# A fixed VectorE order between stages, two weight low parts on GpSimd and a reset bank turn in an encoder kernel

## The chip, the cores and the metric

The kernel runs on one core of a Trainium2 chip. The metric is the device time of one execution in microseconds (us); the time before is the median of three runs. Engines are called by their names in the profile: PE (TensorE), DVE (VectorE), ACT (ScalarE), POOL (GpSimd), SP (the DMA queue's engine).

## The reference, cut to what matters

Two encoder layers on 272 tokens (16 learned meta tokens ahead of 256) of 1024 channels, in float32. Each layer mixes tokens twice in parallel (chunkwise retention and windowed attention), merges both by gates, and then runs a squared-ReLU MLP. Around each half stands a norm before and a norm after:

```
u    = rms_norm(h, norm_mix_pre[l]);  proj = u @ w_in[l]
...
mix  = (sigmoid(gate_r) * y_r + sigmoid(gate_a) * y_a) @ w_mix_o[l]
h    = h + rms_norm(mix, norm_mix_post[l])
u    = rms_norm(h, norm_ff_pre[l])
ff   = square(relu(u @ w_ff1[l])) @ w_ff2[l]
h    = h + rms_norm(ff, norm_ff_post[l])
```

What matters here is the step from one product to the next: the norm after, the addition to `h`, and the input `u` of the next product.

## The kernel before, in words

Channels lie on the 128 partitions, so an activation is eight tiles of 128 channels by 272 tokens (256 in the second layer's later part). Every weight is a unit of 128 x 1024 float32, loaded through three `raw` buffers. To keep float32 precision a unit is split by `unit` (L119): ACT casts it to a high part `wh` (L131), DVE computes the low part `wl = raw - wh` (L132). Both have four buffers, so four units at most lie ready. The activation is split likewise, into `uh` (ACT, L242) and `ul` (DVE, L243, recorded at the helper's line L93). `product` (L146) makes one output tile of 128 channels from one unit: for each of the eight input tiles `mm3` (L135) issues three matmuls into one PSUM bank, wh by uh (L136), wh by ul (L137), wl by uh (L138), in that order in each bank.

Between two stages stands `leave` and then `enter`. `leave` (L296) takes the products out of PSUM (`yg`, ACT), sums squares, lets PE make the mean (L183) and run twenty small matmuls on zeros (`warm`), and gets 1/sqrt on ACT (L189, L190). A Newton step is folded into the update of `h`: its `update(k)` (L312) makes, for tile 0, the tile of `yg`, then `h`, then `y1`, and for every later tile a scaled `yg` and then `h = h + yg`. `held` (L310) makes the fourth weight unit of the next stage be cast on ACT only after the square of the 1/sqrt. `enter` (L225) runs over the eight tiles: `update(k)`, `uh` on ACT, `ul` on DVE, and the sum of squares for the next norm (`accumulate`). There are three such places: mix to ff1 in either layer, and ff2 of layer 0 to the second layer's first products. In the trace they begin at about 251, 447 and 681 us.

No order among these DVE instructions is written down. Each engine runs its instructions in one fixed order, which the framework's scheduler chose from its own estimate of times, save where `tc.issue_after` ties an instruction behind another of the same engine. The order so chosen differs from the code's: in the first place DVE does `y1` before tile 0 of `h`, and takes the later tiles often in pairs.

PSUM banks of the products go round by `wide` (L85): a counter `turn` steps through the tags "asatats" (three banks "a", two "s", two "t"). It runs on through both layers; the first output product (`att_o`, L740) of layer 0 gets "s", the next "a" and "t"; in layer 1 the first gets "a", the second "t". The steps of the retention norm before it use banks "t" and "o" too.

Of the kernel before, what the change touches and what calls it, by code (L numbers as in the profile page):

```python
# [19 lines left out]
KD = D // P  # L20
# [21 lines left out]
def encoder(ctx: ExitStack, tc: tile.TileContext, order, w, h_in, gains, dec, decm, sink, sinkm, tabs, mats, esel, masks, rel, relm, grow, out):  # L42
    nc = tc.nc
    V, A, PE, G = nc.vector, nc.scalar, nc.tensor, nc.gpsimd
    mul, add, sub, mn = ALU.mult, ALU.add, ALU.subtract, ALU.min
# [12 lines left out]
    turn = [0]  # L58
    ring.tile([P, 48], F32, name="gap", bufs=1)

    def slot(i, name, shape=(KD, T), dt=F32):
        return big.tile([P] + list(shape), dt, tag=f"b{i}", name=name)
# [7 lines left out]
    def tokens(i, name, shape=(KD,), at=32):  # L70
        return slot(i, name, (*shape, ROW), F32R)[..., at:at + T]

    def bank(tag, shape=None):
        t = psum.tile([P, 512], F32, tag=tag, name="ps_" + tag, bufs=BANKS[tag])
        if shape is None:
            return t
        n = int(np.prod(shape))
        v = t[:, :n]
        if len(shape) == 2:
            v = v.rearrange("p (a b) -> p a b", a=shape[0])  # L80
        elif len(shape) == 3:
            v = v.rearrange("p (a b c) -> p a b c", a=shape[0], b=shape[1])
        return v

    def wide():  # L85
        turn[0] += 1
        return "asatats"[turn[0] % 7]

    def f(t):
        return t.bitcast(F32)  # L90

    def stt(o, a, s, b, op0=mul, op1=mul):
        V.scalar_tensor_tensor(out=o, in0=a, scalar=s, in1=b, op0=op0, op1=op1)  # L93

    def split(xh, xl, x):
        A.activation(xh, x, AF.Copy)  # L96
# [7 lines left out]
    count = {"load": 0}  # L104
    raws = []
    held = {}

    def fetch(parts=1):
        i = count["load"]
        count["load"] += 1  # L110
        raw = ring.tile([P, D], F32, tag="raw", name="raw", bufs=3)
        n = D // parts
        cuts = [slice(j * n, (j + 1) * n) for j in range(parts)]
        raws.append((raw, cuts))
        for c in cuts:
            nc.sync.dma_start(raw[:, c], w[i][:, c])
            yield

    def unit(*name):  # L119
        i = len(order)  # L120
        order.append(name)
        if not raws:
            list(fetch())
        raw, cuts = raws.pop(0)
        wh = ring.tile([P, D], F32R, tag="wh", name="wh")
        wl = ring.tile([P, D], F32R, tag="wl", name="wl")
        for c in cuts:
            with ExitStack() as later:
                for ins in held.get(i, ()):
                    later.enter_context(tc.issue_after(ins))  # L130
                A.activation(wh[:, c], raw[:, c], AF.Copy)  # L131
                V.tensor_tensor(out=wl[:, c], in0=raw[:, c], in1=f(wh[:, c]), op=sub)  # L132
        return wh, wl

    def mm3(ps, ah, al, bh, bl, first=True, last=True):  # L135
        PE.matmul(ps, ah, bh, start=first, stop=False)  # L136
        PE.matmul(ps, ah, bl, start=False, stop=False)  # L137
        return PE.matmul(ps, al, bh, start=False, stop=last)  # L138
# [36 lines left out]
    def warm(n):  # L175
        ps = bank("t", [P])
        for _ in range(n):
            tc.keep_in_program_order(PE.matmul(ps, idle, idle, start=True, stop=True))

    def mean(parts, c0):  # L180
        ms = bank("o", [T])
        for i, p in enumerate(parts):
            PE.matmul(ms[:, c0:], mat["o1024"], p[:, c0:], start=i == 0, stop=i == len(parts) - 1)  # L183
        return ms

    def rsqrt(y1, ms, c0):
        y = two.tile([P, T], F32, tag="t1", name="y")
        w2 = two.tile([P, T], F32, tag="t2", name="w2")
        A.activation(y[:, c0:], ms[:, c0:], AF.Ln)  # L189
        A.activation(y[:, c0:], y[:, c0:], AF.Exp, scale=-0.5)  # L190
        return y, w2, newton(None if y1 is None else y1[:, c0:], ms[:, c0:], 0.0, y[:, c0:], w2[:, c0:])

    warm(WARM)
    h = const.tile([P, KD, T], F32, name="h")
    g = const.tile([P, DEPTH, 4, KD], F32, name="g")
# [24 lines left out]
    def square(src, c0):  # L220
        sq = two.tile([P, T], F32, tag="sq", name="sq", bufs=3)
        A.activation(sq[:, c0:], src, AF.Square)
        return sq

    def enter(l, n, c0, update):  # L225
        x = [tokens(i, "u" + "hl"[i], at=32 - 16 * l) for i in range(2)]
        ss = one.tile([P, T], F32, tag="ss", name="ss")

        lag = KD if n else LAG0

        def accumulate(k):
            sq = square(h[:, k, c0:], c0)
            if k == 0:
                V.tensor_scalar(out=ss[:, c0:], in0=sq[:, c0:], scalar1=8e-6, scalar2=None, op0=add)
            else:
                V.tensor_tensor(out=ss[:, c0:], in0=ss[:, c0:], in1=sq[:, c0:], op=add)

        for k in range(KD):
            if update:
                update(k)  # L240
            gk = g[:, l, n, k:k + 1]
            A.activation(x[0][:, k, c0:], h[:, k, c0:], AF.Copy, scale=gk)  # L242
            stt(x[1][:, k, c0:], h[:, k, c0:], gk, f(x[0][:, k, c0:]), op1=sub)  # L243
            if k >= lag:
                accumulate(k - lag)
        if update and n == 0:
            for k in range(KD - lag, KD):
                accumulate(k)
        return x, ss, accumulate
# [46 lines left out]
    def leave(l, n, c0, products, init=None):  # L296
        yg = slot(4, "yg")
        ss = one.tile([P, T], F32, tag="ss", name="ss2")
        for m, ps in products:
            sq = square(ps[:, c0:], c0)  # L300
            A.activation(yg[:, m, c0:], ps[:, c0:], AF.Copy, scale=g[:, l, n, m:m + 1])
            if m == 0 and init is None:
                V.tensor_scalar(out=ss[:, c0:], in0=sq[:, c0:], scalar1=8e-6, scalar2=None, op0=add)
            elif m < KD - 1:
                V.tensor_tensor(out=ss[:, c0:], in0=(init if m == 0 else ss)[:, c0:], in1=sq[:, c0:], op=add)
        y1 = one.tile([P, T], F32, tag="rb", name="y1")
        ms = mean([ss, sq], c0)
        warm(10)
        y, w2, sq = rsqrt(None, ms, c0)
        held[len(order) + 3] = [sq.ins]  # L310

        def update(k):  # L312
            yk = yg[:, k, c0:]
            if k == 0:
                V.tensor_tensor(out=yk, in0=yk, in1=y[:, c0:], op=mul)
                stt(yk, w2[:, c0:], 3.0, yk, op0=sub)
                stt(h[:, k, c0:], yk, -0.5, h[:, k, c0:], op1=add)
                stt(y1[:, c0:], w2[:, c0:], 3.0, y[:, c0:], op0=sub)
            else:
                stt(yk, yk, -0.5, y1[:, c0:])  # L320
                V.tensor_tensor(out=h[:, k, c0:], in0=h[:, k, c0:], in1=yk, op=add)

        return update

# [11 lines left out]
    lows, odds = slice(64, 128), (slice(32, 64), slice(96, 128))  # L336
# [26 lines left out]
    for l in range(DEPTH):  # L363
        c0 = 16 * l
        if l == 0:
            u, ss, early = lead()
        else:
            u, ss, _ = enter(l, 0, 0, update)
            early = [proj(u, 0, "asas"[i], "v_r", i) for i in range(4)]
# [191 lines left out]
        if l == 0:  # L561
# [6 lines left out]
            for c in range(4):  # L568
                V.tensor_tensor(
                    out=pmblk.rearrange("p (t c g k) -> p t c g k", t=4, c=4, g=2)[:, :, c],  # L570
                    in0=mat["blk"].rearrange("p (t g k) -> p t g k", t=4, g=2),
                    in1=pm[:, 0:16].unsqueeze(1).unsqueeze(1).to_broadcast([P, 4, 2, 16]),
                    op=mul,
# [163 lines left out]
                A.activation(x[:, c0:], x[:, c0:], AF.Tanh, scale=0.5)  # L737
        tc.keep_in_program_order(A.preload_act_table_set("natural_log_exp_and_others"))

        for m2 in range(4):  # L740
            wh, wl = unit("att_o", m2)
            for i in range(2):
                m = 2 * m2 + i
                ps = bank(wide(), [T])
                for k in range(4):
                    sl = slice((4 * i + k) * P, (4 * i + k + 1) * P)
                    mm3(ps[:, c0:], wh[:, sl], wl[:, sl], ao[:, 0, k, c0:], ao[:, 1, k, c0:], k == 0, k == 3)
                stt(tha[m][:, c0:], tha[m][:, c0:], 1.0, ps[:, c0:], op0=add)
# [9 lines left out]
        def mixed():  # L758
# [4 lines left out]
            for m in range(KD):  # L763
                *_, (_, ps) = pair[m] if m < 2 else product(z, c0, wide(), "mix", m)
                yield m, ps

        update = leave(l, 1, c0, mixed())

        u, ss, accumulate = enter(l, 2, c0, update)
        fs, behind = [], []  # L770

# [7 lines left out]
        for m in range(KF):  # L779
            if m % KD == 0:  # L780
                a, b = ((5, 7), (8, 9), (6, 10), (2, 3))[m // KD]
                low = [tokens(i, "fl", (4,), 32 - c0) for i in ("10a", "10b")] if b == 10 else [tokens(b, "fl", at=32 - c0)]
# [13 lines left out]
        if l == 0:  # L796
# [10 lines left out]
            update = leave(l, 3, c0, ff2(), e2)  # L807
# [180 lines left out]
```

## Time and profile before

| what | value |
|---|---|
| median of 3 runs | 868.79 us (868.16 to 870.78) |
| the profiled execution | 872.21 us, of which the span from first to last instruction is 870.4 us |
| PE busy | 852.1 us (98%) |
| DVE, ACT, POOL busy | 603.2, 559.6 and 49.9 us (69%, 64%, 6%) |
| share of the chain that ended last | PE 81%, DVE 10%, ACT 6% |
| mean granted TensorE clock | 0.996 |

The profile is of one execution. A matmul's busy time overlaps that of the next one, so PE at 98% doesn't say that PE issues at its peak; the distance from one matmul's start to the next one's says it.

### The profile page before, as it was taken

The page shows a single profiled execution, that of the slowest core. Times are in us where ns is not written, and L with a number is a line of the kernel's source. Part 1 is how long each engine was busy: PE and PEld are TensorE (multiplying, and loading weights), DVE is VectorE, ACT ScalarE, POOL GpSimd, SP SyncE. Part 2 cuts the span into 40 slices and gives each one's busy share as a digit, 9 for nine tenths or more (in the row PEclk, how much of TensorE's full clock was granted, in tenths as well). Part 3 has the DMA queues.
Part 4 walks back from the last instruction along what each step waited for, and adds up shares of the span by engine and source line. Part 5 has one row for each costly group of instructions (what it writes and reads, how often), then busy time and mean ns, then how long its engine had stood idle before and what let it go on. Part 6 is the DMA issues. An engine that isn't in the chain of part 4 may idle for free.

```text
span 870.4 us, 16670 instructions
## 1 busy us (share of the span) xinstructions
PE 852.1 (98%) x6514; PEld 819.3 (94%) x6514; DVE 603.2 (69%) x1113; ACT 559.6 (64%) x1034; POOL 49.9 (6%) x113
## 2 busy tenths in 40 slices
PE   9899999999999999999999999999999999999997
PEld 9899999999989999999989999999999999998885
DVE  7889888778768655444469898888776675554544
ACT  7448887666568777444355588886755498783432
POOL 2112220000000000000000122200000000000000
PEclk9999999999999999999999999999999999999999
DMA  8544344445545655556544544444466367666661
GB/s 294 190 123 136 118 135 131 129 155 173 169 143 171 193 173 183 178 175 186 174 121 146 155 129 154 137 139 137 121 197 198 113 214 204 196 200 192 189 193 69
DMA packets 41407, 142.15 MB, mean 163 GB/s; under 512 B 5360, under 2 KB 6256, under 8 KB 41328
## 3 DMA queue, kind: packets, MB, share of 16 engines
q1 hardware_dynamic: 40896, 140.43, 52.1%
q8 instruction: 51, 0.84, 0.4%
q10 hardware_dynamic: 432, 0.66, 0.2%
q14 instruction: 28, 0.23, 0.1%
HBM read 140.02 MB, written 1.05 MB: 162 GB/s over the span
## 4 chain that ended last, share of the span: by engine, by line
PE 81%; DVE 10%; ACT 6%; issue 1%; DMA 1%; POOL 0%; SPq 0%; DVEq 0%; ACTq 0%; POOLq 0%
PE ps_a L136 12%; PE ps_a L137 12%; PE ps_a L138 12%; PE ps_s L138 5%; PE ps_s L137 5%; PE ps_s L136 5%; PE ps_t L136 4%; PE ps_t L137 4%; PE ps_t L138 4%; DVE wl L132 3%; PE ps_a L849 2%; PE ps_s L849 2%; PE ps_s L848 2%; PE ps_a L848 2%; PE ps_a L850 2%; PE ps_s L850 2%
## 5 line engine op out<-in xcount | busy, mean ns | idle before, releaser
L132 DVE TENSOR_TENSOR wl<-raw,wh 128x1024 fp32r<-128x1024 f32 x256 | 312.8, 1223 | 198.9 <-ACT wh L131 197.3
L131 ACT ACTIVATE wh<-raw 128x1024 fp32r<-128x1024 f32 x256 | 269.9, 1058 | 203.1 <-PE ps_a L137 61.6
L136 PE MATMUL ps_a<-uh,wh 128*128 128x272 f32 (+1 forms) x912 | 265.8, 292 | 2.8 <-ACT uh L242 2.8
L138 PE MATMUL ps_a<-uh,wl 128*128 128x272 f32 (+1 forms) x912 | 259.3, 284 | 0.3 <-DVE wl L132 0.3
L137 PE MATMUL ps_a<-ul,wh 128*128 128x272 f32 (+1 forms) x912 | 259.3, 285 | 0.0
L136 PEld LDWEIGHTS ps_a<-uh,wh 128*128 128x128 f32 x912 | 172.7, 189 | 4.7 <-ACT uh L242 3.2
L137 PEld LDWEIGHTS ps_a<-ul,wh 128*128 128x128 f32 x912 | 172.5, 189 | 0.9
L138 PEld LDWEIGHTS ps_a<-uh,wl 128*128 128x128 f32 x912 | 172.4, 189 | 0.7 <-DVE wl L132 0.7
L138 PE MATMUL ps_s<-uh,wl 128*128 128x272 f32 (+1 forms) x184 | 52.0, 283 | 0.3 <-DVE wl L132 0.3
L137 PE MATMUL ps_s<-ul,wh 128*128 128x272 f32 (+1 forms) x184 | 52.0, 282 | 0.0
L136 PE MATMUL ps_s<-uh,wh 128*128 128x272 f32 (+1 forms) x184 | 52.0, 283 | 0.0
L136 PE MATMUL ps_t<-uh,wh 128*128 128x272 f32 (+1 forms) x152 | 43.2, 284 | 1.3 <-ACT uh L242 1.3
L137 PE MATMUL ps_t<-ul,wh 128*128 128x272 f32 (+1 forms) x152 | 43.1, 284 | 0.0
L138 PE MATMUL ps_t<-uh,wl 128*128 128x272 f32 (+1 forms) x152 | 42.8, 282 | 0.0
L138 PEld LDWEIGHTS ps_s<-uh,wl 128*128 128x128 f32 x184 | 34.6, 188 | 0.5 <-DVE wl L132 0.5
L136 PEld LDWEIGHTS ps_s<-uh,wh 128*128 128x128 f32 x184 | 34.8, 189 | 0.0
L137 PEld LDWEIGHTS ps_s<-ul,wh 128*128 128x128 f32 x184 | 34.7, 189 | 0.0
L136 PEld LDWEIGHTS ps_t<-uh,wh 128*128 128x128 f32 x152 | 28.6, 188 | 1.5 <-ACT uh L242 1.5
L137 PEld LDWEIGHTS ps_t<-ul,wh 128*128 128x128 f32 x152 | 28.6, 188 | 0.1
L138 PEld LDWEIGHTS ps_t<-uh,wl 128*128 128x128 f32 x152 | 28.6, 188 | 0.0
L97 DVE TENSOR_TENSOR fl<-ft,fh 128x272 fp32r<-128x272 f32 (+1 forms) x64 | 27.6, 433 | 1.0 <-ACT fh L96 0.9
L96 ACT ACTIVATE fh<-ft 128x272 fp32r<-128x272 f32 (+1 forms) x64 | 27.1, 424 | 1.7
(308 smaller groups left out, 1948.3 us busy)
## 6 DMA issues: line engine op xcount, KB each, us to landing
raw<-in_w SPq DMA_DIRECT2D x256, 512.0 KB, 3.7
leads<-in_w SPq DMA_DIRECT2D x6, 256.0 KB, 5.3
tab<-in_tabs SPq DMA_DIRECT2D x2, 544.0 KB, 6.5
h<-in_h_in SPq DMA_DIRECT2D x3, 272.0 KB, 5.1
out<-yt SPq DMA_DIRECT2D x3, 256.0 KB, 2.1
leads<-in_w ACTq DMA_DIRECT2D x2, 256.0 KB, 3.8
gj<-in_grow SPq DMA_DIRECT2D x1, 512.0 KB, 5.5
mats<-in_mats SPq DMA_DIRECT2D x1, 320.0 KB, 7.2
```

What stands on the lines that cost most here:

```text
L96: A.activation(xh, x, AF.Copy)
L97: V.tensor_tensor(out=xl, in0=x, in1=f(xh), op=sub)
L131: A.activation(wh[:, c], raw[:, c], AF.Copy)
L132: V.tensor_tensor(out=wl[:, c], in0=raw[:, c], in1=f(wh[:, c]), op=sub)
L136: PE.matmul(ps, ah, bh, start=first, stop=False)
L137: PE.matmul(ps, ah, bl, start=False, stop=False)
L138: return PE.matmul(ps, al, bh, start=False, stop=last)
L848: PE.matmul(pss[i], xh, wh[:, sl], start=kk == 0, stop=False)
L849: PE.matmul(pss[i], xh, wl[:, sl], start=False, stop=False)
L850: PE.matmul(pss[i], xl, wh[:, sl], start=False, stop=kk == KF - 1)
```

## The change

It has three parts. First, in `enter`, where an update precedes it, DVE's instructions are tied into one line: `h` of tile 0, `y1`, then for each tile scaled `yg`, `h`, and the low part `ul` of the tile before; the sums of squares join that line. Second, the low parts `wl` of the fourth and fifth weight unit after each `leave` are computed on POOL. Third, `turn` is set to 6 ahead of the first output product of each layer, so that the tags begin with "a", "s", "a", "t" there.

```diff
     def stt(o, a, s, b, op0=mul, op1=mul):
-        V.scalar_tensor_tensor(out=o, in0=a, scalar=s, in1=b, op0=op0, op1=op1)
+        return V.scalar_tensor_tensor(out=o, in0=a, scalar=s, in1=b, op0=op0, op1=op1)
...
+    on_pool = set()
...
-                V.tensor_tensor(out=wl[:, c], in0=raw[:, c], in1=f(wh[:, c]), op=sub)
+                (G if i in on_pool else V).tensor_tensor(out=wl[:, c], in0=raw[:, c], in1=f(wh[:, c]), op=sub)
...
+        line, lows = [], []
+
+        def next_in_line(method, *args, **kw):
+            with ExitStack() as later:
+                if line and update:
+                    later.enter_context(tc.issue_after(line[-1]))
+                line.append(method(*args, **kw).ins)
...
-                V.tensor_tensor(out=ss[:, c0:], in0=ss[:, c0:], in1=sq[:, c0:], op=add)
+                next_in_line(V.tensor_tensor, out=ss[:, c0:], in0=ss[:, c0:], in1=sq[:, c0:], op=add)
...
             if update:
-                update(k)
-            gk = g[:, l, n, k:k + 1]
+                update(k, next_in_line)
             A.activation(x[0][:, k, c0:], h[:, k, c0:], AF.Copy, scale=gk)
-            stt(x[1][:, k, c0:], h[:, k, c0:], gk, f(x[0][:, k, c0:]), op1=sub)
+            low = (x[1][:, k, c0:], h[:, k, c0:], gk, f(x[0][:, k, c0:]))
+            if update:
+                lows.append(low)
+                for low in lows[:-1] if k < KD - 1 else lows:
+                    next_in_line(stt, *low, op1=sub)
+                del lows[:-1]
+            else:
+                stt(*low, op1=sub)
...
         held[len(order) + 3] = [sq.ins]
+        on_pool.update((len(order) + 3, len(order) + 4))
 
-        def update(k):
+        def update(k, put):
             yk = yg[:, k, c0:]
             if k == 0:
                 V.tensor_tensor(out=yk, in0=yk, in1=y[:, c0:], op=mul)
                 stt(yk, w2[:, c0:], 3.0, yk, op0=sub)
-                stt(h[:, k, c0:], yk, -0.5, h[:, k, c0:], op1=add)
-                stt(y1[:, c0:], w2[:, c0:], 3.0, y[:, c0:], op0=sub)
+                put(stt, h[:, k, c0:], yk, -0.5, h[:, k, c0:], op1=add)
+                put(stt, y1[:, c0:], w2[:, c0:], 3.0, y[:, c0:], op0=sub)
             else:
-                stt(yk, yk, -0.5, y1[:, c0:])
-                V.tensor_tensor(out=h[:, k, c0:], in0=h[:, k, c0:], in1=yk, op=add)
+                put(stt, yk, yk, -0.5, y1[:, c0:])
+                put(V.tensor_tensor, out=h[:, k, c0:], in0=h[:, k, c0:], in1=yk, op=add)
...
+        turn[0] = 6
         for m2 in range(4):
             wh, wl = unit("att_o", m2)
```

## Rows read from the trace of the kernel before

**Rows 1.** The page's engines: busy us (share of the span) and instructions.
```profile
PE 852.1 (98%) x6514; PEld 819.3 (94%) x6514; DVE 603.2 (69%) x1113; ACT 559.6 (64%) x1034; POOL 49.9 (6%) x113
```

**Rows 2.** Waits of PE, whole span: us in total, times, longest us.
```profile
PE ps_a L136 <- ACT uh L242: 2.8, 2, 1.4
PE ps_t L136 <- ACT uh L242: 1.3, 1, 1.3
```

**Rows 3.** Timeline of PE, first place: start, us, what, idle before.
```profile
256.46 0.39 PE L136 MATMUL ps_a<-uh,wh 128*128 128x272 f32 x1 [1.39 <-ACT uh L242]
...
257.06 0.36 PE L137 MATMUL ps_a<-ul,wh 128*128 128x272 f32 x1
...
269.16 0.28 PE L138 MATMUL ps_s<-uh,wl 128*128 128x272 f32 x1
```

**Rows 4.** Timeline of DVE, first place.
```profile
254.23 0.44 DVE L167 TENSOR_TENSOR w<-ps_o,w 128x272 f32<-128x272 f32 x1
254.71 0.44 DVE L93 SCALAR_TENSOR_TENSOR yg<-w,yg 128x272 f32<-128x272 f32 x1
255.07 0.43 DVE L93 SCALAR_TENSOR_TENSOR y<-w,y 128x272 f32<-128x272 f32 x1
255.42 0.43 DVE L93 SCALAR_TENSOR_TENSOR h<-yg,h 128x272 f32<-128x272 f32 x1
...
256.48 0.49 DVE L93 SCALAR_TENSOR_TENSOR ul<-h,g,uh 128x272 fp32r<-128x272 f32 x1
...
262.83 1.21 DVE L132 TENSOR_TENSOR wl<-raw,wh 128x1024 fp32r<-128x1024 f32 x1
...
267.49 2.46 DVE L132 TENSOR_TENSOR wl<-raw,wh 128x1024 fp32r<-128x1024 f32 x2
```

**Rows 5.** Timeline of ACT, first place.
```profile
254.10 1.04 ACT L131 ACTIVATE wh<-raw 128x1024 fp32r<-128x1024 f32 x1
255.89 0.52 ACT L242 ACTIVATE uh<-h,g 128x272 fp32r<-128x272 f32 x1 [0.74 <-DVE h L93]
...
266.39 1.06 ACT L131 ACTIVATE wh<-raw 128x1024 fp32r<-128x1024 f32 x1 [0.37 <-PE ps_a L137]
```

**Rows 6.** Windows of PE: stretch, length, PE busy (count), clock, DMA share, GB/s.
```profile
257.05:268.90 11.85, 11.85 (x94) 1.00 0.16 46
267.05:268.90 1.85, 1.85 (x17) 1.00 0.08 20
452.57:465.29 12.72, 12.44 (x94) 1.00 0.14 43
463.37:465.29 1.92, 1.92 (x17) 1.00 0.50 198
686.67:697.95 11.28, 11.28 (x94) 1.00 0.15 48
696.36:697.95 1.59, 1.59 (x16) 1.00 0.10 34
```

**Rows 7.** Timeline of PE where the output products of layer 1 begin.
```profile
627.11 0.38 PE L136 MATMUL ps_t<-ao,wh 128*128 128x256 f32 x1 [0.28 <-DVE vw L93]
```

**Rows 8.** Timeline of POOL: its longest write, one scaling alone and one beside DVE.
```profile
2.75 1.00 POOL L329 MEMSET ql<- 128x1088 f32 x1
...
71.77 0.44 POOL L594 TENSOR_SCALAR pmk<-ex,rs 128x64 f32<-128x64 f32 x1 [1.09 <-DVE rs L557]
...
510.76 1.59 POOL L594 TENSOR_SCALAR pmk<-ex,rs 128x64 f32<-128x64 f32 x1 [0.37 <-DVE rs L557]
```

**Rows 9.** Timeline of DVE beside the last of these.
```profile
510.59 1.21 DVE L132 TENSOR_TENSOR wl<-raw,wh 128x1024 fp32r<-128x1024 f32 x1
511.71 0.86 DVE L528 TENSOR_TENSOR ql<-t,qk 64x256 fp32r<-64x256 f32 x2
```

**Rows 10.** Windows of PE where the granted clock fell (columns of Rows 6).
```profile
40.00:44.00 4.00, 1.78 (x13) 1.00 0.52 147
44.00:48.00 4.00, 4.00 (x22) 0.57 0.35 123
```

More of the change, by code (lines that the diff above doesn't have):

```diff
@@ L233, in accumulate @@
             if k == 0:
-                V.tensor_scalar(out=ss[:, c0:], in0=sq[:, c0:], scalar1=8e-6, scalar2=None, op0=add)
+                next_in_line(V.tensor_scalar, out=ss[:, c0:], in0=sq[:, c0:], scalar1=8e-6, scalar2=None, op0=add)
             else:
-                V.tensor_tensor(out=ss[:, c0:], in0=ss[:, c0:], in1=sq[:, c0:], op=add)
+                next_in_line(V.tensor_tensor, out=ss[:, c0:], in0=ss[:, c0:], in1=sq[:, c0:], op=add)
         for k in range(KD):
+            gk = g[:, l, n, k:k + 1]
             if update:
-                update(k)
-            gk = g[:, l, n, k:k + 1]
+                update(k, next_in_line)
             A.activation(x[0][:, k, c0:], h[:, k, c0:], AF.Copy, scale=gk)
-            stt(x[1][:, k, c0:], h[:, k, c0:], gk, f(x[0][:, k, c0:]), op1=sub)
+            low = (x[1][:, k, c0:], h[:, k, c0:], gk, f(x[0][:, k, c0:]))
[6 more added lines that the diff above has]
+                stt(*low, op1=sub)
             if k >= lag:
```

## The prediction

> **What bounds the kernel now.** I read the page's engines first: PE is busy 98% of the span, so the end is set by PE, and an edit is worth only what it adds to or takes from PE's idle time [rows 1]. The list of PE's waits comes next: of all of them the three waits for `uh`, one at each place between two stages, are the largest, 4.1 us together [rows 2]. Then I read the first place instruction by instruction. PE stands idle 1.39 us until tile 0 of `uh` arrives, does one matmul in each of its four banks, and at 257.06 goes on with the first `ul` [rows 3]. DVE runs without a pause there: the start of an instruction that needs the one before it comes 0.48 us after that one (254.23 to 254.71), of another 0.35 to 0.36 us (254.71 to 255.07, 255.07 to 255.42) [rows 4]. ACT has the fourth weight's high part ready at 255.14, but DVE makes its low part only at 262.83 [rows 4, 5]. Last, the windows tell how far PE is from its pace. In the first place 92 matmuls begin within 11.85 us (94 in the window, two of which were running): 0.1288 us each, where 15 undisturbed ones right behind take 1.85, 0.1233 each. So 0.50 us are lost in small waits. The second place gives 12.72 / 92 = 0.1383 against 1.92 / 15 = 0.128, a loss of 0.95; the third 0.1226 against 0.1136, a loss of 0.83 [rows 6]. Everything that a better order behind the first `ul` can win is their sum, 2.28 us.
>
> **The line on DVE.** Tile 0 of `h` now follows its `yg` directly: 254.71 + 0.48 = 255.19 in place of 255.42, so `uh` and PE's first four matmuls come 0.23 us sooner [rows 3 to 5]. Those four are all that PE can do, because in each bank the second matmul needs `ul`. And `ul` of tile 0 now stands behind `y1` (255.54), `yg` of tile 1 (needs `y1`, 256.02) and `h` of tile 1 (256.50): 256.85 in place of 256.48. The first matmul on `ul` came 0.58 us after that instruction's start, so it moves from 257.06 to 257.43, 0.37 us later. From then on DVE needs per tile 0.48 + 0.35 + at most 0.49 = 1.32 us, PE 12 x 0.1233 = 1.48: DVE stays ahead and the small waits should go. In the second place a sum of squares adds 0.35 to the later four tiles, 1.67 against 12 x 0.128 = 1.54, some 0.5 us in all, which the lead from the tiles before covers. The part is worth 3 x 0.37 - 2.28 = -1.2 us. Its bounds are +1.1 (no small wait goes) and -3.0 (all go, and the 0.23 us is kept three times).
>
> **The fourth weight's low part on POOL.** DVE loses an instruction of 1.21 us [rows 4], which is counted already: its gap is one of the small waits. POOL gets it at about 255.2, in the middle of DVE's chain, where nearly every instruction reads two operands from SBUF. What that does is the main question. POOL's scaling of 128x64 takes 0.44 us alone, and 1.59 us when DVE is at a `wl` (two operands from SBUF) and then at two `ql` [rows 8, 9]. So POOL doesn't get at its data while such DVE instructions run one into the next, and gets through when they pause. The trace has no long POOL read that DVE meets, so the reverse is bounded: below by nothing (DVE goes on; that `wl` took its usual 1.21), above by three passes over 1024 elements. POOL writes 1088 elements in 1.00 us [rows 8], so a pass is about 0.94 and three are 2.8, an estimate. I take two passes, one for each operand, 1.8 us, since it is reading that collides. DVE's first pause is at 255.97, between `y1` and the `yg` that needs it. If POOL gets in there, that `yg`, every `h` and `ul` queued behind it, ACT's `uh` and then PE's matmuls all come 1.8 us later: PE has nothing to do from 256.7 to 259.2. Idle time of PE isn't won back: 3 x 1.8 = +5.4 us.
>
> The Trainium skill states such a rule ("SBUF — State Buffer", section Who interferes with whom): a DVE instruction with two SBUF inputs and a GpSimd one that reads SBUF exclude each other, and whichever comes second is blocked for the whole of the other. The trace agrees for DVE ahead of POOL (0.44 us became 1.59) and shows no long case of the reverse. The skill's "GPSIMD Engine Reference" (section 3.1) has 4497 ns for a two-input operation of 2048 elements; half of it, an estimate, is 2.25 us, by which the sum would be 1.35 us higher.
>
> **The fifth weight's low part.** Its cast ends at 267.45 [rows 5]; DVE starts it at 267.49 (the first of two in 2.46 us, so done at about 268.7), and PE needs it at 269.16 [rows 3, 4]. POOL with two passes ends at about 269.4, 0.25 us too late, 3 x 0.25 = +0.75. Bounds: 0, if PE has other matmuls ahead, and 3 x 1.2, if POOL first has to sit out one of DVE's `wl`. The next `wl` on DVE may come later in turn; PE has 24 matmuls, 3 us, ahead of it, which hides that. No DMA is moved; the fourth `raw` comes free sooner, the fifth some tenths later, and nothing in the waits hangs on it.
>
> **The bank turn.** In layer 1 the second output product waits 0.28 us for its bank "t" [rows 7]; with "s" it doesn't: -0.3. In layer 0 "a" replaces "s" for the first one, with three banks to choose from: nothing, at worst the same 0.3 back.
>
> **The clock.** Once in this trace, from 40 to 44 us, PE was busy only 1.78 of 4 us, and in the next 4 us the granted clock was 0.57 of 2.4 GHz on average: mostly the lower level, 1.2 GHz. There 21 matmuls began in place of 4 / 0.1233 = 32, a loss of 1.4 us [rows 10]. In the forecast PE does four matmuls between the end of the zeros' product, about 255, and 259.2. That is emptier than the stretch shown, while the 1.39 us of before left the clock alone. Bounds are no fall and three, 0 to 4.2 us; I take one, 1.4.
>
> **The sum.** -1.2 + 5.4 + 0.75 - 0.3 + 1.4 = +6.1 us. The profiled execution (872.2, span 870.4) would become 878.3; it lies 3.4 us above the median of 868.8, which becomes 874.9.
>
> **Rivals.** *They don't block each other.* POOL reads beside DVE, or lets it through; for it speaks that the `wl` beside POOL's scaling was not longer than others. Then the line, the bank and at most some of the fifth weight count: 868.8 - 1.2 - 0.3 = 867.3, not slower. It decides where POOL holds DVE for less than (1.2 + 0.3 - 0.75) / 3 = 0.25 us a place. Chance 0.34; most of it lies within 0.3%, which is about what a measurement of this kernel can tell from no change (2.6 us), and 0.12 below, where all small waits go.
>
> *DVE keeps the way.* POOL gets only the pauses of 0.13 us, and reads after DVE's chain, which by the pace above ends near 264.7. The low part is then there at about 266.6 in place of 264.04, and PE, whose order is fixed, waits at the fourth product: 3 x 2.5 - 1.5 = +6.0, 874.8. For it speaks that POOL sat out three DVE instructions [rows 8, 9]; against, that the chain now has a pause in every tile. Chance 0.12.
>
> *It does less than it says.* POOL's hold is short or partly hidden by a different order of PE's matmuls, and gains and losses cancel: 868 to 870. Chance 0.10.
>
> **How the numbers follow.** The forecast has 0.44, of which 0.04 within 0.3% (one pass of 0.94 us and no fall: +1.3). Alone it reaches from 870 to 880. Faster: 0.12. Same: 0.04 + 0.22 + 0.10 = 0.36. Slower: 0.40 + 0.12 = 0.52. The range has to hold the first rival too: 866.3 leaves out only its lowest end, 879 three falls with three passes.
>
> **What would show it.** Right: in the changed profile POOL has six TENSOR_TENSOR of 128x1024; in each place a DVE instruction on `yg` or `h` is 1 to 2 us long where its fellows take 0.43, or has that much idle before it, and PE waits as long for `ul` or `uh`. A fallen clock shows as a PEclk under 1.00 in the windows behind. `h` of tile 0 begins before `y1`, and the wait for bank "t" is gone. Wrong: DVE's instructions keep 0.41 to 0.49 us while POOL's run beside them (then the first rival), or POOL's takes 5 us and more and PE waits for `wl` (the second). If the first `ul` is not 0.37 us later against `uh`, the step on the line fails.

## The result, and the profile after

The changed kernel takes 883.64 us (883.24 to 884.30, 4 runs), the kernel before beside it 869.78: a ratio of 1.0155 [1.0133, 1.0177], 13.9 us slower. The forecast was 874.9 with a range to 879.0: the side is right, the size less than half.

The page's engines and the group of POOL's new instructions (xcount | busy, mean ns of one | idle before):

```profile
PE 854.3 (97%) x6514; PEld 820.8 (93%) x6514; DVE 609.1 (69%) x1107; ACT 561.3 (64%) x1034; POOL 66.2 (8%) x119
...
L133 POOL TENSOR_TENSOR wl<-raw,wh 128x1024 fp32r<-128x1024 f32 x6 | 14.9, 2488 | 291.9 <-DVE yg L93 132.9
```

DVE has six instructions fewer than in [rows 1] and yet is busy 5.9 us longer. Six `wl` of some 1.2 us are gone, so what remains is busy 13 us longer. The first place shows which: DVE, then POOL (start, us, what), both with the same two columns ahead.

```profile
252.72 0.44 DVE L93 SCALAR_TENSOR_TENSOR h<-yg,h 128x272 f32<-128x272 f32 x1
253.08 2.60 DVE L93 SCALAR_TENSOR_TENSOR y<-w,y 128x272 f32<-128x272 f32 x1
...
256.55 0.49 DVE L93 SCALAR_TENSOR_TENSOR ul<-h,g,uh 128x272 fp32r<-128x272 f32 x1
```

```profile
252.77 2.61 POOL L133 TENSOR_TENSOR wl<-raw,wh 128x1024 fp32r<-128x1024 f32 x1 [127.24 <-DVE yg L93]
267.77 2.41 POOL L133 TENSOR_TENSOR wl<-raw,wh 128x1024 fp32r<-128x1024 f32 x1 [12.38 <-PE ps_t L139]
```

`y1` took 0.43 us before [rows 4] and takes 2.60 here; it ends at 255.68, 0.30 us after POOL's instruction (255.38). Everything in the line stands behind it. PE in the same place, and its waits over the whole span (us in total, times, longest):

```profile
253.77 0.39 PE L137 MATMUL ps_t<-uh,wh 128*128 128x272 f32 x1 [1.16 <-ACT uh L250]
...
257.10 0.59 PE L138 MATMUL ps_t<-ul,wh 128*128 128x272 f32 x1 [2.57 <-DVE ul L93]
```

```profile
PE ps_t L138 <- DVE ul L93: 5.1, 2, 2.6
PE ps_a L138 <- DVE ul L93: 2.6, 1, 2.6
PE ps_t L137 <- ACT uh L250: 2.2, 2, 1.2
PE ps_o L184 <- DVE ss L237: 1.8, 1, 1.8
...
PE ps_a L137 <- ACT uh L250: 1.2, 1, 1.2
```

The waits for `uh` [rows 2] are a little shorter, the waits for `ul` are new, once at each place, and so is one of 1.8 us for the sum that the mean is made from: in the second place POOL's second low part runs from 468.95 for 2.38 us, and DVE's last two sums, from 469.23, take 2.95. Behind each stall the granted clock fell (stretch, length, PE busy (count), clock, DMA share, GB/s):

```profile
256.50:260.10 3.60, 3.00 (x13) 0.53 0.43 137
454.50:461.50 7.00, 5.25 (x23) 0.51 0.25 75
696.80:700.40 3.60, 3.60 (x20) 0.53 0.22 88
```

A mean of 0.53 is the 1.2 GHz level for nearly the whole window. In the trace of before no place shows it; its only fall ahead of the end is that of [rows 10].

**Where the time went.** The table gives how late PE is against the first trace of before, counted from the first warming matmul of each place (252.68, 448.19 and 682.44 us there), at the 108th matmul (the stream of the stage's first products) and at the 200th (behind the fifth weight and the mean). Further columns: PE's idle time at the place (gaps between starts within 6.5 us of that first matmul), and how long the granted clock stood at half within 12 us. The kernels are those of the experiments below.

| kernel | at 108th, us | at 200th, us | idle, us | at half, us |
|---|---|---|---|---|
| before | 0 | 0 | 1.5, 1.5, 1.4 | none |
| before, profiled again | -0.01, 0, 0.01 | -0.01, 0.09, 0.01 | 1.5, 1.5, 1.4 | none |
| bank alone | 0, 0.01, 0 | 0, 0.09, 0 | 1.5, 1.5, 1.4 | none |
| after | 3.43, 3.80, 3.38 | 3.64, 6.15, 3.90 | 4.0, 4.0, 3.9 | 3.4, 6.8, 3.4 |
| after, profiled again | 3.52, 3.85, 4.42 | 3.74, 6.13, 4.93 | 4.1, 4.0, 3.9 | 3.4, 6.8, 6.8 |
| fourth weight alone | 3.27, 2.60, 1.87 | 3.27, 3.03, 1.87 | 3.7, 4.0, 3.6 | 3.4, 3.4, 0 |
| fifth weight alone | 0, 0, 0 | 0.94, 1.39, 1.52 | 1.5, 1.5, 1.4 | none |
| line and bank | 2.62, 2.00, 2.22 | 2.62, 3.04, 2.22 | 3.0, 3.3, 2.8 | 3.4, 3.4, 3.4 |
| low part last | 0.66, 1.15, 0.67 | 0.66, 6.45, 1.07 | 1.9, 1.9, 1.7 | 0, 3.4, 0 |
| first `ul` early | 0.85, 1.29, 0.86 | 0.85, 7.77, 1.27 | 1.9, 1.9, 1.8 | none |
| POOL only writes | 0.29, -0.47, 0.33 | 0.29, 1.49, 0.74 | 1.9, 1.9, 1.7 | none |
| POOL copies early | 1.69, 0.88, 0.25 | 2.00, 2.89, 0.25 | 1.9, 1.9, 1.7 | 3.4, 3.4, 0 |
| sums free | 0.31, 0.89, 0.28 | 0.31, 1.33, 0.28 | 1.9, 1.9, 1.8 | 0, 3.4, 0 |
| POOL copies beside the line | 2.34, 1.71, 1.12 | 2.34, 4.09, 1.12 | 2.7, 2.7, 2.6 | 3.4, 3.4, 0 |
| POOL writes beside the line | 1.52, -0.45, 0.34 | 1.52, 1.51, 0.75 | 1.9, 1.9, 1.8 | 3.4, 0, 0 |
| interleaved line | 2.20, 1.42, 2.12 | 2.20, 1.43, 2.12 | 1.3, 1.3, 1.2 | none |

For the changed kernel the 200th matmuls add up to 3.64 + 6.15 + 3.90 = 13.7 us, about the difference of the medians. With the kernel in which POOL only writes as the line alone (its order of matmuls is the changed kernel's in the first and third place, and for the first 154 in the second), they part as follows. The line to the 108th: 0.29 - 0.47 + 0.33 = +0.15. The hold: the first `ul` matmul comes 6.88 us after the first warming one in the first place, 4.72 where POOL only writes, so 2.16, and as much in the others: 6.5. The rest at the 108th is the clock: 0.98 + 2.10 + 0.89 = 4.0. That is what is left over; what a fall costs by itself stands in the section on the prediction. From the 108th to the 200th, the fifth weight with the wait for the mean: 0.21 + 2.35 + 0.52 = 3.1. Hold, clock and fifth part are all larger than forecast, and the line gives nothing.

### The profile page after: what moved, and what is told of

It is laid out like the page before. It is cut to its first block, busy times and chain, and to the rows that moved or that the text cites. A ratio compares the mean times of both kernels' runs of the same rounds, so it can differ in the third digit from the quotient of the medians.

```text
span 881.5 us, 16675 instructions
## 1 busy us (share of the span) xinstructions
PE 854.3 (97%) x6514; PEld 820.8 (93%) x6514; DVE 609.1 (69%) x1107; ACT 561.3 (64%) x1034; POOL 66.2 (8%) x119
## 4 chain that ended last, share of the span: by engine, by line
PE 79%; DVE 11%; ACT 6%; issue 2%; DMA 1%; POOL 0%; POOLq 0%; SPq 0%; DVEq 0%; ACTq 0%
PE ps_a L138 12%; PE ps_a L139 12%; PE ps_a L137 12%; PE ps_t L138 4%; PE ps_s L139 4%; PE ps_s L138 4%; PE ps_t L139 4%; PE ps_t L137 4%; PE ps_s L137 4%; DVE wl L133 3%; PE ps_a L866 2%; PE ps_a L865 2%; PE ps_a L867 2%; ACT wh L132 1%; DMA leads<-in_w 1%
## 5 line engine op out<-in xcount | busy, mean ns | idle before, releaser
L133 DVE TENSOR_TENSOR wl<-raw,wh 128x1024 fp32r<-128x1024 f32 x250 | 307.8, 1233 | 202.6 <-ACT wh L132 201.3
L138 PE MATMUL ps_t<-ul,wh 128*128 128x272 f32 (+1 forms) x168 | 48.4, 288 | 5.1 <-DVE ul L93 5.1
L137 PE MATMUL ps_t<-uh,wh 128*128 128x272 f32 (+1 forms) x168 | 48.2, 287 | 2.2 <-ACT uh L250 2.2
L139 PE MATMUL ps_t<-uh,wl 128*128 128x272 f32 (+1 forms) x168 | 48.1, 286 | 0.0
L138 PEld LDWEIGHTS ps_t<-ul,wh 128*128 128x128 f32 x168 | 32.5, 193 | 5.5 <-DVE ul L93 5.5
L133 POOL TENSOR_TENSOR wl<-raw,wh 128x1024 fp32r<-128x1024 f32 x6 | 14.9, 2488 | 291.9 <-DVE yg L93 132.9
L137 PE MATMUL ps_a<-fh,wh 128*128 128x272 f32 x128 | 36.7, 286 | 0.0
L138 PE MATMUL ps_a<-fl,wh 128*128 128x272 f32 x128 | 36.7, 286 | 0.0
L139 PE MATMUL ps_a<-fh,wl 128*128 128x272 f32 x128 | 36.7, 286 | 0.0
L137 PEld LDWEIGHTS ps_t<-uh,wh 128*128 128x128 f32 x168 | 32.4, 193 | 2.6 <-ACT uh L250 2.6
```

What stands on the lines that cost most here:

```text
L133: (G if i in on_pool else V).tensor_tensor(out=wl[:, c], in0=raw[:, c], in1=f(wh[:, c]), op=sub)
```

## The experiments

**The line and the bank, without POOL.**

```diff
-        on_pool.update((len(order) + 3, len(order) + 4))
```

> The change without its POOL part: the line on DVE and the bank turn stay, the fourth and fifth low parts go back to DVE. Theory H (POOL's low part holds DVE, the rest of the change is worth little): 867 to 869.5 us, y1 on DVE 0.43 us again in place of 2.6, PE's wait for the first ul at most 0.7 us at each place, no fall of the clock at the three places. Theory L (the line itself delays PE: ul behind h of the next tile, the sums tied in): 876 us or more, PE still waits over 2 us for ul at each place.

877.7 us, 1.0082 [1.0061, 1.0104]: not what I had expected of my own theory. DVE in the first place, and PE's waits:

```profile
254.42 1.22 DVE L133 TENSOR_TENSOR wl<-raw,wh 128x1024 fp32r<-128x1024 f32 x1
255.56 0.43 DVE L93 SCALAR_TENSOR_TENSOR h<-yg,h 128x272 f32<-128x272 f32 x1
```

```profile
PE ps_t L137 <- ACT uh L250: 3.4, 2, 2.3
PE ps_a L137 <- ACT uh L250: 2.3, 1, 2.3
PE ps_t L138 <- DVE ul L93: 1.8, 2, 1.4
```

With a line in which each instruction waits for its predecessor, the scheduler finds a pause at its very head and puts the fourth weight's low part in, ahead of `h` (in the third place behind `y1`). Before, it stood at 262.83 [rows 4]. So this run says what the line costs when that low part stays on DVE untied, not what the line costs. Moving the low part to POOL is what keeps the head of the line clear, and POOL then blocks it in another way.

**One weight alone, in the order of before.**

The second kernel has `+ 4` in the same line.

```diff
+        on_pool.add(len(order) + 3)
```

> The kernel before with the fourth weight's low part on POOL and nothing else changed. Theory H: at each place one DVE instruction of the chain takes about 2.6 us, PE loses 2 to 2.7 us there and the granted clock falls behind it, 1.5 to 1.7 us more each time: 878 to 883 us. Theory L: 868 to 872 us, DVE's instructions at the places keep 0.41 to 0.49 us.

879.21 us, 1.0102 [1.008, 1.0124]. DVE, POOL, and PE's waits:

```profile
253.35 0.43 DVE L93 SCALAR_TENSOR_TENSOR y<-w,y 128x272 f32<-128x272 f32 x1
253.70 2.58 DVE L93 SCALAR_TENSOR_TENSOR h<-yg,h 128x272 f32<-128x272 f32 x1
```

```profile
253.51 2.47 POOL L133 TENSOR_TENSOR wl<-raw,wh 128x1024 fp32r<-128x1024 f32 x1 [127.24 <-DVE yg L93]
```

```profile
PE ps_a L137 <- ACT uh L243: 7.1, 2, 3.5
PE ps_t L137 <- ACT uh L243: 3.4, 1, 3.4
```

The hold needs no line: it hits whichever instruction is next, here `h` itself, so that PE waits for `uh` 3.5 us instead of 1.4. Again DVE's instruction ends 0.30 us after POOL's (256.28, 255.98).

> The kernel before with the fifth weight's low part on POOL and nothing else changed. Theory H: POOL runs when DVE has wl and sums to do; one DVE instruction there takes 2.3 to 2.4 us, PE feels it only at the second place (the mean of the squares late by about 1.8 us) and as some tenths for the late low part at the others: 870 to 873 us, no fall of the clock at the first and third place. Theory L: 869 to 870 us.

874.88 us, 1.0052 [1.0032, 1.0073]: more than either theory gave. DVE and POOL in the second place, and PE's waits:

```profile
462.64 2.47 DVE L237 TENSOR_TENSOR ss<-ss,sq 128x272 f32<-128x272 f32 x1 [0.60 <-ACT sq L223]
```

```profile
462.43 2.38 POOL L133 TENSOR_TENSOR wl<-raw,wh 128x1024 fp32r<-128x1024 f32 x1 [18.60 <-ACT wh L132]
```

```profile
PE ps_o L184 <- DVE ss L237: 1.1, 1, 1.1
...
PE ps_a L139 <- POOL wl L133: 0.9, 1, 0.9
...
PE ps_s L139 <- POOL wl L133: 0.7, 1, 0.7
```

In the second place the held instruction is the sum that the mean waits for; in the other two a `wl` of 2.30 us (1.21 before), and PE waits for POOL's own low part. The first place, DVE and then POOL:

```profile
266.44 2.30 DVE L133 TENSOR_TENSOR wl<-raw,wh 128x1024 fp32r<-128x1024 f32 x1 [1.36 <-ACT wh L132]
```

```profile
265.27 2.39 POOL L133 TENSOR_TENSOR wl<-raw,wh 128x1024 fp32r<-128x1024 f32 x1 [139.54 <-ACT wh L132]
```

This longer instruction ends 1.08 us after POOL's (268.74, 267.66), not 0.30. Both are the instruction's usual time less 0.13 (1.21 and 0.43): a held instruction does nearly all its work after POOL's end.

**The bank alone.**

```diff
+        turn[0] = 6
         for m2 in range(4):
```

> The kernel before with the bank turn set to 6 ahead of the output products and nothing else changed. Both theories: 0.3 to 0.5 us less, 869.3 us, which the runs can hardly tell from no change; in the trace PE's wait for bank t behind vw, 0.28 us at the first output products of layer 1, is gone.

869.63 us, 0.9994 [0.9979, 1.0009]: no difference that can be measured. The wait of [rows 7] is gone in its trace as in that of after.

**The low part tied behind the line.** In both kernels POOL is out; in the second the first `ul` stands right behind `y1`.

```diff
+        if update:
+            held[len(order) + 3].append(line[-1])
```

> The changed kernel with no low part on GpSimd, and VectorE's low part of the fourth weight tied behind the last residual low part of the line, so that it can't stand in the line's head as it did in the kernel with the line and the bank alone (254.42, 452.56, 688.38 us there). Theory M (the line itself costs nothing; what cost 8 us there was the 1.22 us low part in a pause of the line, and the clock falls that its stall set off): 866 to 870.5, PE's waits for uh at the places about 1.2 us each instead of 2.3, no fall of the granted clock at the places. Rival O (the fixed order itself is what costs: the first ul comes a tile later): 873 to 878, the waits for ul of 1.4 to 2.6 us stay, and at least two of the three falls with them.

> As the kernel just above, and the first residual low part goes into the line right behind y1 instead of behind tile 1's two instructions. Theory M: 865.5 to 870, PE's wait for the first ul at each place under 0.9 us, so up to 1 us a place less than the kernel above and no clock falls. Rival O (any fixed order costs, whichever): 873 to 878. If the kernel above has no waits for ul over 0.9 us, the two are the same within 0.2%.

879.74 us, 1.0119 [1.0086, 1.0153], and 882.52 us, 1.0144 [1.0118, 1.0171]. Both expectations fell. The first and third place lose 0.7 to 0.9 us to the 108th matmul; the second loses 5.3 and 6.5 us more between the 108th and the 200th. The first kernel's waits from 455 to 480 us, and its DVE:

```profile
PE ps_t L448 <- DVE vt L441: 4.1, 1, 4.1
```

```profile
465.15 0.98 DVE L237 TENSOR_TENSOR ss<-ss,sq 128x272 f32<-128x272 f32 x2
466.95 1.23 DVE L133 TENSOR_TENSOR wl<-raw,wh 128x1024 fp32r<-128x1024 f32 x1 [0.83 <-ACT wh L132]
...
472.55 0.44 DVE L441 SCALAR_TENSOR_TENSOR vt<-ps_a,rb 128x272 f32<-128x272 f32 x1
```

The held low part (461.03) and the two behind it stand ahead of DVE's last sum, three more between that sum and `vt`, which attention needs. Behind this wait the granted clock falls again, at 472.58 here and at 473.95 in the second kernel, so that the 5.3 and 6.5 us hold a fall each. Neither place that was tried for the low part is free: at the head it delays `h`, behind the line `vt` of the second place.

**The line with a POOL that doesn't read.** In the first kernel POOL writes zeros in place of the subtraction, in the second it copies `raw` (`G.tensor_copy(wl[:, c], raw[:, c])`); the two weights' low parts are left out, or lack the subtraction.

```diff
+                if i in on_pool:
+                    G.memset(f(wl[:, c]), 0.0)
+                else:
+                    V.tensor_tensor(out=wl[:, c], in0=raw[:, c], in1=f(wh[:, c]), op=sub)
```

> The changed kernel, with GpSimd writing a constant into the two low parts in place of the subtraction (it leaves out these two weights' low parts): GpSimd runs an instruction at the same points that writes 128x1024 and reads nothing. Theory H1 (DVE is held by GpSimd's reads of two operands, which it shares with VectorE): y1 stays at 0.43 us, GpSimd's instruction takes 0.8 to 1.3 us, 866 to 871. Rival H2 (any GpSimd instruction holds DVE for its length): y1 takes 0.9 to 1.4 us, about 1 us a place and no or one clock fall: 871 to 876.

> The changed kernel, with GpSimd copying the weight into the low part in place of the subtraction (it leaves out the subtraction of the high part in these two weights): one operand read instead of two. Theory H1 (only an instruction with two operands holds DVE): y1 0.43 us, 866 to 871, whatever the copy takes. Rival H2 (any GpSimd read or write holds DVE for its whole length): y1 as long as the copy, 1.0 to 2.5 us, and 873 to 884 by that length.

873.34 us, 1.0037 [1.002, 1.0054], and 873.16 us, 1.0044 [1.0022, 1.0066]. As a test of the hold they missed: without `wh` as an operand POOL runs 3 us earlier (at 250.10 and 249.11), before the line begins. But they are the line alone, with no low part in it and no hold. The line's first `ul` comes at 4.72 us instead of 4.38, and then (windows of PE in the writing kernel, each from the first `ul` to the start of the 93rd matmul):

```profile
255.80:267.62 11.82, 11.81 (x93) 1.00 0.15 44
451.60:463.53 11.93, 11.92 (x93) 1.00 0.09 26
685.08:696.41 11.33, 11.32 (x93) 1.00 0.15 42
```

92 matmuls take 11.81, 11.92 and 11.32 us, where before had 11.85, 12.72 and 11.28 [rows 6]: only the second place wins. Over half of its 0.80 us isn't the order's: before waited there for the fourth weight's low part, 0.58 us from start to start (461.06 to 461.64) where 0.125 to 0.128 is usual, and the writing kernel doesn't compute that low part. Before:

```profile
461.64 0.40 PE L138 MATMUL ps_s<-uh,wl 128*128 128x272 f32 x1 [0.28 <-DVE wl L132]
```

Why the small waits stay shows in the first place, DVE's `ul` of tile 3 and then PE's matmul on it:

```profile
258.98 0.49 DVE L93 SCALAR_TENSOR_TENSOR ul<-h,g,uh 128x272 fp32r<-128x272 f32 x1
```

```profile
259.53 0.39 PE L141 MATMUL ps_t<-ul,wh 128*128 128x272 f32 x1
```

The `ul` ends at 259.47, PE begins 0.06 us later, and PE's next matmul follows after 0.23 us instead of 0.12: PE waited for `ul`, in a gap too small for the list of waits. Much the same stands at tiles 0, 5 and 7 (0.05 to 0.11 us). From the first matmul on tile 0's `ul` to this one there are 29, so 9.7 a tile and not 12: 1.19 us, and DVE's line needs 1.24 a tile.

The second place loses its gain again behind the mean. Waits of the writing kernel from 455 to 480 us, its DVE ahead of `vt`, and that of before:

```profile
PE ps_t L450 <- DVE vt L443: 1.3, 1, 1.3
```

```profile
466.91 1.22 DVE L136 TENSOR_TENSOR wl<-raw,wh 128x1024 fp32r<-128x1024 f32 x1
468.06 0.43 DVE L443 SCALAR_TENSOR_TENSOR vt<-ps_a,rb 128x272 f32<-128x272 f32 x1
```

```profile
468.39 0.44 DVE L424 SCALAR_TENSOR_TENSOR vt<-ps_a,rb 128x272 f32<-128x272 f32 x1
```

DVE does a `wl` of a later weight just ahead of `vt`, behind `rb`, the instruction that `vt` needs (466.49); before does `rb` at 467.92 and `vt` right behind it. That `wl` stands there in all four kernels whose POOL only writes or copies and whose sums are tied, not in the changed kernel. The 0.41 us in the third place, from the 108th to the 200th, are TensorE's pace in that execution (see the end of this section): 92 matmuls at 117.8 ns instead of 113.3.

**The sums out of the line, second place.** As the writing kernel (the two low parts are left out), with `next_in_line` for the sums only where `n` isn't 0.

> The kernel in which GpSimd only writes (it leaves out the two low parts), with the sums of squares of the second place taken out of the line. Theory S (that kernel's second place loses 2 us because the line sets each sum behind a later tile, so that the three buffers of squares come free late, ScalarE's last square falls behind two weights' high parts, and the mean and vt come 5 us later than before): the last sum by 461 to 463 instead of 465.8, no wait for vt over 0.5 us, 871 to 873 (2 us less in the second place, the rest as it was). Rival (the line's pace of 1.24 us a tile makes the sums late, wherever they stand): the wait for vt of 1.4 us stays, 873 to 875.

871.83 us, 1.0033 [1.0009, 1.0057]. The time alone doesn't tell the two kernels apart, since this execution had a fall of the clock at the second place. From the 108th to the 200th matmul it loses 0.44 us, where the writing kernel lost 1.96. The same wait, and `vt`:

```profile
PE ps_t L456 <- DVE vt L449: 0.2, 1, 0.2
```

```profile
469.97 0.44 DVE L449 SCALAR_TENSOR_TENSOR vt<-ps_a,rb 128x272 f32<-128x272 f32 x1
```

That looks like theory S, but the trace doesn't bear it out. `vt` is no earlier: it begins 21.30 us behind the place's first warming matmul (469.97 - 448.67), in the writing kernel 21.17 (468.06 - 446.89). The wait is short because PE comes later, by 1.36 us at the 108th matmul (0.89 against -0.47), where the clock fell. Nor were the tied sums late: the writing kernel's last sum begins 16.13 us behind the first warming matmul (463.02 - 446.89), that of before 16.62 (464.81 - 448.19), the free one 14.02. With the sums free no `wl` stands between `rb` (469.49) and `vt`. What the tied sums cost stays open.

**What POOL must do to hold DVE.** Here POOL's instruction waits for `wh`, as in the change. It copies `wh`, or copies one column of it and then writes the other 1,023 (the two low parts are left out in both).

```diff
+                    G.tensor_copy(wl[:, c], f(wh[:, c]))
```

```diff
+                    first = G.tensor_copy(wl[:, 0:1], f(wh[:, 0:1]))
+                    with tc.issue_after(first.ins):
+                        G.memset(f(wl[:, 1:D]), 0.0)
```

> The changed kernel, with GpSimd copying the high part into the low part instead of subtracting (it leaves out these two weights' low parts): the copy waits for wh as the subtraction did, so that it runs beside the line, but reads one operand; some 1.04 us long (what GpSimd's copy of a weight took in the run before). Theory H1 (VectorE is held only by a GpSimd instruction with two operands): h and y1 stay at 0.44 us and the first ul comes by 255.5. Rival H2 (any read of GpSimd holds VectorE for its length): one of h, y1 and yg takes 0.9 to 1.4 us at each place, and the first ul comes 0.5 to 1.0 us later than in the kernel where GpSimd only wrote (254.90 + 0.36 + about 0.5).

> As the kernel above, but GpSimd copies only the first column of the high part and then writes a constant into the other 1,023 (it leaves out the two low parts): a write of 0.95 us beside the line, with no operand. Theory H1 and also H2: no instruction of VectorE over 0.5 us in the line's head. Rival H3 (any GpSimd instruction holds VectorE): one of them takes 0.8 to 1.3 us. If both this and the copy leave VectorE alone, two operands are what counts.

877.51 and 874.69 us, one run each. The copying kernel's DVE and POOL:

```profile
253.48 1.27 DVE L93 SCALAR_TENSOR_TENSOR y<-w,y 128x272 f32<-128x272 f32 x1
```

```profile
253.14 1.31 POOL L134 CAST wl<-wh 128x1024 fp32r<-128x1024 f32 x1 [127.21 <-DVE yg L93]
```

The writing kernel's:

```profile
253.74 0.43 DVE L93 SCALAR_TENSOR_TENSOR y<-w,y 128x272 f32<-128x272 f32 x1
254.20 0.44 DVE L93 SCALAR_TENSOR_TENSOR yg<-yg,y 128x272 f32<-128x272 f32 x1
```

```profile
253.80 0.95 POOL L136 MEMSET wl<- 128x1023 f32 x1
```

A single operand holds DVE for POOL's whole instruction (`y1` ends at 254.75, POOL at 254.45), and a write of the same size beside the same instructions doesn't. So it is POOL's reading, and its length is POOL's length: H1 falls for the copy, H3 for the write. The Trainium skill has this rule ("SBUF — State Buffer", section Who interferes with whom): a DVE instruction with two SBUF inputs contends with a GpSimd one that reads SBUF, not with one that only writes. All four runs agree, with 0.43 us grown to 2.60, 2.58 and 1.27, and 0.43 left alone.

**Warming over the stall.** The changed kernel with `warm(28)` for `warm(10)`.

> The changed kernel with 28 warming matmuls at each place instead of 10: they end at about 256.1 instead of 252.3, the first four matmuls still come before the first ul at 257.1, so that PE's wait becomes busy time and nothing starts later. Theory C (PE's idle time at the places brings the falls of the granted clock, 3.4, 6.8 and 3.4 us at half): no fall at the places, and 875 to 879, as the falls cost about half their length (6.8 us in all), less what the queue behind the warming loses. Rival (the falls come whatever PE does there, or cost nothing): falls at the places stay, 882 to 886.

889.01 us, 1.0201 [1.0167, 1.0235]: slower still. The granted clock stays up at the first two places; it falls at 479.7, behind a wait for `vt` of 2.3 us, and at 701.5 in the third place. But filling the stall wins nothing. The 300th matmul behind the warming comes 4.91 us late against before in the first place, where it was 3.64 in the changed kernel: the warming's last matmul ends at 257.1, in place of 252.6, the scheduler ordered PE's matmuls anew behind it, and PE waits three times for `ul`, 1.5 us together. So a filled stall kept its clock in two places of three; what a fall costs this run can't say.

**An order meant to be better.** No POOL; per tile `yg`, `ul` of the tile before, `h`, so that no instruction follows the one that it reads; sums free.

```diff
                 put(stt, yk, yk, -0.5, y1[:, c0:])
+                put(stt, *lows.pop(), op1=sub)
                 put(V.tensor_tensor, out=h[:, k, c0:], in0=h[:, k, c0:], in1=yk, op=add)
```

> A better order, without GpSimd: for each tile yg, then the low part of the tile before, then h (so that no instruction of the line follows the one that it reads), the sums of squares free, the fourth weight's low part behind the line's last low part (after the sixth tile's in the second place), and the bank. Theory L (what the line cost was the 0.11 us between dependent neighbours, 1.24 us a tile against PE's 1.23, and the sums tied to its end): 866.5 to 869.5, the first ul 0.3 us earlier than in the kernel with the low part tied last, no wait for vt after the second place. Rival (any fixed order loses to the scheduler's own): 872 to 878.

874.98 us, 1.0058 [1.0039, 1.0077]. The head is as planned: the first matmul on `ul` comes 4.25 us behind the first warming one, 0.13 earlier than before. Then the free sums get between the tiles in all three places, DVE needs 1.47 us a tile, and PE loses 2.2, 1.4 and 2.1 us in gaps of some 0.1 us that the list of waits doesn't show one by one. No version beat the kernel before.

**Both kernels profiled once more.**

> The changed kernel once more, for what its two profiled executions have in common. If the falls of the granted clock belong to the stalls, all three places show one again; the double fall of the second place and the pace of TensorE in the last two stretches (117.8 ns a matmul from 639 to 681, 113.4 from 696 to 782 us) may come out otherwise. 882 to 885.5.

> The kernel before once more. If TensorE's pace in a stretch (117.8 ns a matmul from 630 to 675, 113.4 from 690 to 775 us in the first profile) belongs to the kernel, it is the same again; if it belongs to the execution, it may change, with 1.8 us for the first and 3.4 us for the second stretch. No fall of the granted clock at the places, in either case. 867.8 to 874.

884.78 and 868.68 us. The changed kernel has a fall at each place again, now of double length in the second and the third; before has none at a place. TensorE's pace in a stretch belongs to the execution. The first trace of before and the second (columns as above):

```profile
640.00:670.00 30.00, 30.00 (x257) 1.00 0.66 196
700.00:770.00 70.00, 70.00 (x620) 1.00 0.70 210
```

```profile
640.00:670.00 30.00, 30.00 (x267) 1.00 0.72 218
```

And the kernel in which POOL only writes:

```profile
700.00:770.00 70.00, 70.00 (x596) 1.00 0.64 196
```

In the first stretch the same matmuls of the same kernel run at 117 ns each in one execution and at 112 in the other, with the granted clock at 1.00, which is 1.1 us in these 30. The second stretch shows the same two values between kernels whose order of matmuls is alike there; that those too belong to the execution is likely, not shown.

## Why the prediction was right or wrong

**The hold: right mechanism, size and place off.** The step said that POOL gets in at DVE's first pause, between `y1` and `yg`, and holds it 1.8 us. It gets in one instruction earlier, between `h` and `y1`, where DVE makes no pause (0.36 us from start to start), and holds DVE until its own end: 2.16 us a place, 6.5 together instead of 5.4. Two passes of a write were too short for POOL's reading: it takes 2.38 to 2.61 us. The Trainium skill's "GPSIMD Engine Reference" (section 3.1), whose 4497 ns for 2048 elements make 2.25 us by half, an estimate, was nearer. The first rival (no blocking) is excluded by the runs with one weight alone. The second (POOL must wait for DVE's chain) too: POOL went first each time.

**The clock: price right, count wrong.** This term is the largest single miss. I took one fall of 1.4 us out of a range of none to three, though the forecast put the same stall at all three places. There were three, one or two of them of double length, for 4.0 us. That the stalls bring them is supported by the table: with 2.6 us and more of PE's idle time at a place there was a fall in 13 of its 15 cases, with 1.2 to 1.6 us in none of 15, with 1.7 to 1.9 in 5 of 18. A clean test is lacking: the longer warming changed PE's order too, and the clock fell in its third place all the same, with 1.7 us of waits for `ul`. What one costs is seen where the same order of matmuls ran with and without: first place, 1.69 and 1.52 against 0.29, second place 0.88 against -0.47, so 1.2 to 1.4 us for 3.4 us at half. In the changed kernel 0.9 to 1.0 is left for each single one. Why it was double in the second place both times stays open.

**The line: wrong in its gain.** The first `ul` 0.37 us later was right (0.34). The step that failed is "PE 12 x 0.1233 = 1.48: DVE stays ahead and the small waits should go". PE does 9.7 matmuls a tile there, 1.19 us, and the line's 1.24 keep it waiting. Of 2.28 us the writing kernel wins back 0.80, all in the second place, and over half of that because a low part is left out; the other places have 0.04 and -0.04. So the line is worth +0.15 us to the 108th matmul, with that gain in it, rather than -1.2. In the four kernels whose POOL only writes or copies, with the sums tied, the second place then loses 2.0 to 2.4 us more, with a wait of 0.9 to 1.3 for `vt` behind a `wl` that the scheduler set ahead of it; the changed kernel has no such wait. Whether the line or the low parts left out brought that `wl` there isn't settled.

**The fifth weight: too small.** The forecast was 0.75 of a range to 3.6. In the change it costs 3.1; alone 0.94 + 1.39 + 1.52 = 3.9, of which 0.4 in the third place is TensorE's pace. The step asked only whether POOL's low part comes too late, not what DVE instruction POOL holds meanwhile: a `wl`, or, in the second place, the sum that the mean needs, for 2.35 of the 3.1.

**The bank:** -0.3 forecast; too small to be measured. "Does less than it says" is excluded by the size.

So the sum went from 6.1 to 13.7: the hold +1.1, the clock +2.6, the fifth weight +2.35, the line +1.35, and the bank's 0.3. Three falls and the measured hold alone would have made 878.6, within the range; the line and the fifth weight took it out.

## What to carry to other kernels

Before moving an elementwise instruction to GpSimd, ask whether it reads SBUF while VectorE runs two-operand instructions on the path: in these runs each such read stopped VectorE until GpSimd's instruction ended, and a write didn't. What a VectorE instruction with one operand in SBUF does beside such a read was not tried. A stall that is put into TensorE's stream is paid again when the granted clock falls behind it, so price it at every place where it stands. How many matmuls PE has while VectorE makes one tile is read from the order in the trace: here 9.7, where the code suggested 12. An order tied by hand leaves pauses for whatever isn't tied: look at what the scheduler puts there, and at who waits for the line's last instruction.

## What was not expected of the hardware

TensorE's pace at a granted clock of 1.00 has two values, which hold for a whole stretch of 30 us and more: 30 / 257 = 0.117 and 30 / 267 = 0.112 us a matmul in two executions of one kernel. What sets it is open. VectorE, when held, does nearly all of the instruction after GpSimd's end: a 128x272 one of 0.43 us ended 0.30 us after it in four cases, a `wl` of 1.21 us 1.08 after it.
